# Queries and keys of retention's first head as a fifth group of the seven-product stage, by way of DRAM, and that head's retention unit in a queue of its own

## The chip, the cores and the metric

The kernel runs on one core of one Trainium2 chip. The metric is the time on the device in microseconds, the median of the runs. The kernel before: 2191.88 us, median of 3 runs (2191.68 to 2192.81). A smaller number is better.

## The reference

One transformer block on 512 tokens of width 2048, in float32. A normalized input is projected by `w_in`; the columns are the queries of eight attention heads, keys and values of three kinds, gates, and for four retention heads of width 256 queries, keys, values and gates. Sparse attention (compressed, selected and windowed keys) and retention give a mixture, which `w_out` projects; an MLP follows.

```python
h = rms_norm(x, norm_mix_pre[l])
proj = h @ w_in[l]
q_a, kv_a, gate_a, q_r, k_r, v_r, g_r = jnp.split(proj, IN_OFFSETS, axis=-1)
...
k_cmp = compress_kv(kv6[:, :, 0], cmp_pe_k[l], cmp_w1_k[l], cmp_b1_k[l], cmp_w2_k[l])
v_cmp = compress_kv(kv6[:, :, 1], cmp_pe_v[l], cmp_w1_v[l], cmp_b1_v[l], cmp_w2_v[l])
...
q_r = rope(q_r.reshape(B, S, RET_HEADS, RET_DK), pos)
k_r = rope(k_r.reshape(B, S, RET_HEADS, RET_DK), pos)
o_r = retention(q_r, k_r, v_r.reshape(B, S, RET_HEADS, RET_DV), log_gamma)
o_r = (jax.nn.silu(g_r.astype(jnp.float32)) * o_r.reshape(B, S, RET_WIDTH)).astype(x.dtype)
mix = jnp.concatenate([o_a.astype(x.dtype), o_r], axis=-1) @ w_out[l]
```

The retention heads are independent of each other: each needs the scores of its rotated queries and keys, times a decay table, then the product with its values, a normalization over its 256 outputs, and its gate.

## The kernel before, in words

Every product with a weight matrix is made of three matmuls. `split` makes of a float32 operand a rounded part (a copy on ScalarE, line 143) and a rest (a subtraction on VectorE, line 144); `mm3` (lines 155 to 157) multiplies high by high, high by low and low by high into one PSUM bank.

A projection by `w_in` is done in one of two ways.

*Direct blocks.* A block has 512 columns of `w_in`, in eight slabs (`Slab`) of 256 rows. A slab is loaded on SyncE's queue and split; `Driver.run` keeps two slabs split ahead. A step multiplies one slab into four PSUM banks, so a block is 32 pieces of six matmuls of 512 columns. After each piece the driver calls `pump`, which puts a little other work behind it; on its engine every instruction then runs in the order in which it was written. `feat_major` gives features by tokens (queries and keys, which `qk_done` copies into the tile QK), `tok_major` gives tokens by features (values and gates, `vg_done`).

*The seven-product stage.* A group is two column ranges of 256, split in two by rows and by tokens, and is computed with seven products instead of eight (Strassen's scheme in Winograd's form). `Feed` loads the quarters of the weights, sums them on VectorE (line 357) or in an accumulating DMA on GpSimd's queue (line 323), and splits them (lines 362 and 339). `groups` (line 709) runs seven products of 48 matmuls of 256 columns for a group; `in_done` puts the results together on VectorE and stores them as two halves in DRAM, `pd[n, 0]` and `pd[n, 1]`, by ScalarE's queue (line 677). The table `INC` lists the groups: one of keys and values for the compressor, one of other keys, two of attention queries.

After that stage come the direct blocks of the retention heads, queries and keys, then values and gates, for head 0 to 3 (blocks are counted from the one of values ahead of the stage, so that the first of these is block 2). Beside them, in the pumps, run the units of the object `side`: two calls of `compress` (keys, then values), loads, eight attention units (`nsa_unit`) for each of two key groups, and four retention units (`ret_unit`). A unit has two generators: the first computes scores, the second mixes. `Side.step` moves the second generator of an earlier unit and the first of a later one by one step each per piece; a first may be at most one unit ahead. A unit can be held back until the driver has reached a block (`after(n)`). `drain` runs units to their ends with no pieces between.

What a retention unit does: its first generator rotates QK on VectorE (lines 1013 to 1020, twelve operations of 128x512 in six steps), loads its decay table `dec` by GpSimd's queue (line 1023), and makes four score products into the PSUM bank `S` (line 1030), each multiplied by `dec` into the tile AT on VectorE (line 1032). Its second generator does, four times, a gate (`sg`, lines 1040 to 1043: an exponential on ScalarE, three operations on VectorE), output matmuls into the bank `oT` (line 1065), a normalization on VectorE with a power on GpSimd (lines 1069 to 1073, 161 and 162), and two transposes of the result (line 1048).

An attention unit writes each of its scores into the same single bank `S` (line 906), from where VectorE reads it (line 907, and line 897 for the compressed scores, `Pc`); then come maxima (924, 925, 931), exponentials, the scaling of the probabilities (939 to 945), transposes (970, 974) and products. `compress` transposes its position table, does 32 matmuls with the weights `w1s` (line 813) in four pieces, transposes the result (825), and makes a GELU from it on VectorE and ScalarE (the tile z, lines 826 to 838). The two halves of `w1s` have one buffer each: the value weights are loaded, by GpSimd's queue (line 799), when the matmuls with the key weights are done with a half.

GpSimd's queue starts its DMAs in the order written; each waits for its own conditions, and those behind it wait with it. The attention stage ends with the line that sets how far the driver and the units run:

```python
for blocks, units, firsts, pump in ((2, 0, 0, every), (3, 0, 0, every), (4, 7, 8, every), (5, 8, 0, every),
                                    (6, 12, 13, every), (7, 13, 0, every), (8, 22, 22, every)):
    drv.run(blocks * B - 1, pump=pump)
    side.drain(units, firsts)
    drv.run(blocks * B, pump=pump)
```

Of the kernel before, what the change touches and what calls it, by code (L numbers as in the profile page):

```python
# [10 lines left out]
F32 = mybir.dt.float32  # L11
# [5 lines left out]
P = 128  # L17
S = 512
# [5 lines left out]
HR, DR = 4, 256  # L24
# [8 lines left out]
OFF_KV = HA * DK  # L33
# [79 lines left out]
def block_kernel(ctx: ExitStack, tc: tile.TileContext, x, norm_mix_pre, w_in, cmp_pe_k, cmp_w1_k, cmp_b1_k,  # L113
# [488 lines left out]
    more = [ip.tile([P, SL], F32, name=f"half{i}") for i in range(5)]  # L602
    INC = [(OFF_KV, OFF_KV + 256), (OFF_KV + 512, OFF_KV + 1024), (0, 256), (512, 768)]
    G_KV, G_K, G_Q0, G_Q1 = range(4)
    pd = dram.tile([len(INC), 2, P, SL], F32, name="pd")

# [144 lines left out]
    drv.run()  # L751
    next_up = slabs_of(w_in, [(OFF_QR, DR), (OFF_KR, DR)], pool_a)
    for n, _ in enumerate(groups()):
# [250 lines left out]
    AT0 = [0, 512, 896, 1152]  # L1004

    def ret_unit(h):
        def scores():
            QK = RT["qk", h]
            for f in (0, 2):
                x1, x2 = QK[:, f, :], QK[:, f + 1, :]  # L1010
                t1 = rp.tile([P, S], F32, name="rt", bufs=2)
                t2 = rp.tile([P, S], F32, name="rt", bufs=2)
                nc.vector.tensor_mul(t1, x1, rot[:, 1, :])
                nc.vector.tensor_mul(t2, x2, rot[:, 1, :])
                yield
                nc.vector.tensor_mul(x1, x1, rot[:, 0, :])
                nc.vector.tensor_mul(x2, x2, rot[:, 0, :])
                yield
                nc.vector.tensor_sub(x1, x1, t2)
                nc.vector.tensor_add(x2, x2, t1)  # L1020
                yield
# [65 lines left out]
    def proj(cols, done, tok=False):  # L1087
        sl = next_up if cols[0][0] == OFF_QR else slabs_of(w_in, cols, pool_a)
        n = sum(c for _, c in cols)
        drv.steps += tok_major(sl, n, done) if tok else feat_major(sl, n // P, done)  # L1090

    for h in range(HR):
        proj([(OFF_QR + h * DR, DR), (OFF_KR + h * DR, DR)], qk_done(h))
        proj([(OFF_VR + h * DR, DR), (OFF_GR + h * DR, DR)], vg_done(h), tok=True)
    B = NSLAB
    two = lambda c: side.step() if c % 2 else None
    three = lambda c: side.step() if c else None
    every = lambda c: side.step()
    after = lambda n: (lambda: drv.at > n * B)
# [11 lines left out]
    for u in range(8):  # L1111
        if u == 4:
            side.add(*ret_unit(0), after(2), after(3))
        side.add(*nsa_unit(0, u // 2, u % 2))
    side.add(*ret_unit(1), after(4), after(5))
    for u in range(8):
        if u == 6:
            side.add(*ret_unit(2), after(6), after(7))
        side.add(*nsa_unit(1, u // 2, u % 2))
    side.add(*ret_unit(3), after(8))  # L1120
    kv_load()
    compress_load(0)
    for blocks, units, firsts, pump in ((2, 0, 0, every), (3, 0, 0, every), (4, 7, 8, every), (5, 8, 0, every),
                                        (6, 12, 13, every), (7, 13, 0, every), (8, 22, 22, every)):
        drv.run(blocks * B - 1, pump=pump)
        side.drain(units, firsts)
        drv.run(blocks * B, pump=pump)
    actx.close()
# [32 lines left out]
    for s in range(NSLAB):  # L1161
        drv.run(8 * B + s + 1, pump=lambda c: side.first() if c % 2 else None)
        if s:
# [5 lines left out]

    drv.run(10 * B - 1, pump=lambda c: side.second() if c % 2 else None)  # L1170
    side.drain()
    drv.run(12 * B)
    rctx.close()
# [8 lines left out]
    for s in range(NSLAB):  # L1182
        wend[s].load()
        drv.run(12 * B + s + 1)
    wctx.close()
# [574 lines left out]
```

## Time and profile before

| what | us |
|---|---|
| median of 3 runs | 2191.88 |
| span of the profiled execution | 2191.4 |
| TensorE busy in it | 2142.3 |
| VectorE busy | 1632.9 |
| ScalarE busy | 1018.5 |
| seven-product stage, four groups (75.0 to 231.0) | 156.0 |
| first direct block after it, queries and keys of head 0 (231.0 to 293.6) | 62.6 |
| second, values and gates of head 0 (293.6 to 355.2) | 61.6 |
| third (355.2 to 429.2) | 74.0 |
| fourth (429.2 to 496.5) | 67.3 |

The profile gives for each engine its busy time and, for each instruction, its start, its length, and what ended the idle time before it. In the rows that follow, PE is TensorE's matmul, PEld its weight load, DVE VectorE, ACT ScalarE, POOL GpSimd, SP SyncE; ACTq and POOLq are their DMA queues. A name such as `S<-QK` is output from input, and L with a number is a line of the kernel. Matmuls are pipelined, so that the listed length of one is more than its distance from the next; the rate is read from the count in a stretch of time. A direct block takes longer than its own matmuls because the units' matmuls stand between them.

### The profile page before, as it was taken

To read this page: it belongs to the slowest core of one execution; us is meant where nothing else is said; L and a number is where in the kernel's file an instruction comes from. 1 tells how busy PE (TensorE), PEld (TensorE's weight loads), DVE (VectorE), ACT (ScalarE), POOL (GpSimd) and SP (SyncE) were. 2 spreads that over 40 slices of the span, in tenths; PEclk is the share of its full clock that TensorE was granted. 3 is DMA by queue.
4 is the path that set the end of the run, shared out by engine and by line. 5 is a ranking of instruction groups with operands and counts; after the bars stand their busy time and mean duration, and the time that the engine had idled before them with its cause. 6 is when DMAs were issued, how large, how long until landed. Compare 5 with 4: busy or idle time off the path is not lost.

```text
span 2191.4 us, 33442 instructions
## 1 busy us (share of the span) xinstructions
PE 2142.3 (98%) x13363; PEld 1921.7 (88%) x13363; DVE 1632.9 (75%) x1925; ACT 1018.5 (46%) x1469; POOL 153.2 (7%) x175
## 2 busy tenths in 40 slices
PE   8999999999999999999999999999999999999996
PEld 7999887778778899999999999999888888888875
DVE  6987346656665543588888877777878999999997
ACT  5544233333433323475554555555664454445453
POOL 1000210010000000000000000000000000000011
PEclk9999999999999999999999999999999999999998
DMA  6876842243223334577877757676785657567575
GB/s 193 214 199 167 278 126 64 75 106 97 60 78 115 107 102 134 175 237 202 231 220 204 210 163 205 167 206 185 226 240 161 209 154 219 161 187 207 167 232 110
DMA packets 275310, 372.15 MB, mean 170 GB/s; under 512 B 16683, under 2 KB 190811, under 8 KB 274001
## 3 DMA queue, kind: packets, MB, share of 16 engines
q1 hardware_dynamic: 209040, 265.00, 38.6%
q0 software_dynamic: 38736, 59.91, 14.8%
q10 hardware_dynamic: 27378, 45.11, 5.6%
q8 instruction: 105, 1.72, 0.3%
q14 instruction: 51, 0.42, 0.1%
HBM read 321.92 MB, written 48.04 MB: 169 GB/s over the span
## 4 chain that ended last, share of the span: by engine, by line
PE 86%; DVE 7%; DMA 3%; ACT 2%; issue 2%; POOL 0%; SPq 0%; DVEq 0%; ACTq 0%; POOLq 0%
PE prod L156 17%; PE prod L157 17%; PE prod L155 17%; PE mm L155 10%; PE mm L157 10%; PE mm L156 10%; DVE wlo L339 2%; PE S L906 2%; DMA raw<-in_w_in 1%; PE S L1030 1%; PE PT L970 1%; PE oT L1065 1%; PE oT L813 1%; PE oT L155 1%; DMA xh<-ud 1%
## 5 line engine op out<-in xcount | busy, mean ns | idle before, releaser
L362 ACT CAST whi<-Y 128x1024 fp32r<-128x1024 f32 x227 | 238.2, 1050 | 282.1 <-PE prod L157 118.4
L156 PE MATMUL prod<-wlo,Hh 128*128 128x512 f32 x896 | 350.3, 391 | 4.4 <-DVE wlo L339 4.3
L155 PE MATMUL prod<-whi,Hh 128*128 128x512 f32 x896 | 349.4, 390 | 1.4 <-ACT whi L362 1.4
L362 ACT CAST whi<-low 128x1024 fp32r<-128x1024 f32 x215 | 226.3, 1054 | 267.1 <-PE prod L157 135.7
L157 PE MATMUL prod<-whi,Hl 128*128 128x512 f32 x896 | 349.3, 390 | 0.0
L339 DVE TENSOR_TENSOR wlo<-Y,whi 128x1024 fp32r<-128x1024 f32 x227 | 276.7, 1220 | 52.3 <-ACT whi L362 51.4
L339 DVE TENSOR_TENSOR wlo<-low,whi 128x1024 fp32r<-128x1024 f32 x215 | 262.0, 1220 | 56.0 <-ACT whi L362 55.3
L157 PE MATMUL prod<-Hh,wlo 128*128 128x256 f32 x1024 | 284.6, 278 | 4.9 <-DVE wlo L339 4.9
L155 PE MATMUL prod<-Hh,whi 128*128 128x256 f32 x1024 | 285.0, 278 | 0.3 <-ACT Hh L143 0.3
L156 PE MATMUL prod<-Hl,whi 128*128 128x256 f32 x1024 | 284.2, 278 | 0.9 <-DVE Hl L144 0.9
L155 PE MATMUL mm<-whi,Hh 128*128 128x416 f32 (+4 forms) x704 | 264.2, 375 | 0.7 <-ACT Hh L143 0.7
L157 PE MATMUL mm<-whi,Hl 128*128 128x416 f32 (+4 forms) x704 | 248.5, 353 | 0.7 <-DVE Hl L144 0.7
L156 PE MATMUL mm<-wlo,Hh 128*128 128x416 f32 (+4 forms) x704 | 247.7, 352 | 0.0
L144 DVE TENSOR_TENSOR wlo<-raw,whi 128x1024 fp32r<-128x1024 f32 (+4 forms) x120 | 129.3, 1083 | 157.2 <-ACT whi L143 156.5
L155 PE MATMUL prod<-sx,whi 128*128 128x256 f32 x768 | 212.2, 276 | 0.0
L157 PE MATMUL prod<-sx,wlo 128*128 128x256 f32 x768 | 212.2, 276 | 0.0
L156 PE MATMUL prod<-sx,whi 128*128 128x256 f32 x768 | 212.2, 276 | 0.0
L143 ACT CAST whi<-raw 128x1024 fp32r<-128x1024 f32 (+4 forms) x120 | 111.9, 936 | 205.3 <-PE mm L157 104.9
L156 PEld LDWEIGHTS prod<-wlo,Hh 128*128 128x128 f32 x896 | 168.6, 188 | 42.5 <-DVE wlo L339 7.6
L155 PEld LDWEIGHTS prod<-whi,Hh 128*128 128x128 f32 x896 | 168.5, 188 | 37.1 <-ACT whi L362 1.9
L157 PEld LDWEIGHTS prod<-whi,Hl 128*128 128x128 f32 x896 | 168.6, 188 | 34.7
L157 PEld LDWEIGHTS prod<-Hh,wlo 128*128 128x128 f32 x1024 | 193.0, 188 | 5.6 <-DVE wlo L339 5.5
(321 smaller groups left out, 4420.9 us busy)
## 6 DMA issues: line engine op xcount, KB each, us to landing
low<-in_w_up SPq DMA_DIRECT2D x76, 512.0 KB, 4.8
raw<-in_w_in SPq DMA_DIRECT2D x144, 256.0 KB, 3.1
Y<-in_w_up SPq DMA_DIRECT2D x64, 512.0 KB, 4.8
low<-in_w_down SPq DMA_DIRECT2D x64, 512.0 KB, 4.9
Y<-in_w_down SPq DMA_DIRECT2D x64, 512.0 KB, 4.7
Y<-ud SPq DMA_DIRECT2D x49, 512.0 KB, 8.1
ud<-Y ACTq DMA_DIRECT2D x77, 256.0 KB, 5.2
half<-in_w_in SPq DMA_DIRECT2D x27, 512.0 KB, 4.8
```

The costliest lines, as they stand in the source:

```text
L143: nc.scalar.copy(hi, src)
L144: nc.vector.tensor_sub(lo, src, hi.bitcast(F32))
L155: nc.tensor.matmul(ps, ah, bh, start=first, stop=False, skip_group_check=more)
L156: nc.tensor.matmul(ps, ah, bl, start=False, stop=False, skip_group_check=more)
L157: nc.tensor.matmul(ps, al, bh, start=False, stop=last, skip_group_check=more)
L339: nc.vector.tensor_sub(lo, src, hi.bitcast(F32))
L362: nc.scalar.copy(hi, src)
L813: nc.tensor.matmul(hid[:65, :DK], kv[:, l:l + STRIDE * 64 + 1:STRIDE], w1s[l // 16][:, l % 16, :], start=l == 0, stop=l == CBLK - 1)
L906: nc.tensor.matmul(sps[:, :c + L], QT[g][:, h, qs], k, start=True, stop=True)
L970: nc.tensor.transpose(pt[:, e * P:(e + 1) * P], Pt[:, e, rows_of(j)], ident)
L1030: nc.tensor.matmul(sps[:, :n], QK[:, 2 + d, rows_of(j)], QK[:, d, j * P:], start=d == 0, stop=d == 1)
L1065: nc.tensor.matmul(o[:, :DR], AT[:, a0:a0 + P], vr[:, j, :], start=j == 0, stop=j == i)
```

## The change

Queries and keys of head 0 become the fifth entry of `INC` and go through the seven-product stage; the direct block for them goes, and every later block has a number less by one. The result comes back from DRAM by two loads on GpSimd's queue (`qk_load`), called ahead of the first block, behind the loads of the compressor's key weights. The retention unit of head 0 leaves `side` and is the only unit of a second queue, `front`, which is moved by one step after each piece too, from the first piece on; its first eight steps do nothing. Its outputs may begin when the block of its values is done, as before. The table of the last loop is written anew for the lower block numbers, with a pair for `front.drain`.

```diff
-    INC = [(OFF_KV, OFF_KV + 256), (OFF_KV + 512, OFF_KV + 1024), (0, 256), (512, 768)]
-    G_KV, G_K, G_Q0, G_Q1 = range(4)
+    INC = [(OFF_KV, OFF_KV + 256), (OFF_KV + 512, OFF_KV + 1024), (0, 256), (512, 768), (OFF_QR, OFF_KR)]
+    G_KV, G_K, G_Q0, G_Q1, G_R0 = range(5)
...
-    next_up = slabs_of(w_in, [(OFF_QR, DR), (OFF_KR, DR)], pool_a)
+    next_up = slabs_of(w_in, [(OFF_VR, DR), (OFF_GR, DR)], pool_a)
...
+    def qk_load():
+        QK = RT["qk", 0] = rp.tile([P, 4, S], F32, name="QK")
+        for j in range(2):
+            nc.gpsimd.dma_start(QK[:, 2 * j:2 * j + 2, :].rearrange("p f n -> p (f n)"), pd[G_R0, j])
+
     def ret_unit(h):
         def scores():
             QK = RT["qk", h]
+            if not h:
+                for _ in range(8):
+                    yield
...
     for h in range(HR):
-        proj([(OFF_QR + h * DR, DR), (OFF_KR + h * DR, DR)], qk_done(h))
+        if h:
+            proj([(OFF_QR + h * DR, DR), (OFF_KR + h * DR, DR)], qk_done(h))
         proj([(OFF_VR + h * DR, DR), (OFF_GR + h * DR, DR)], vg_done(h), tok=True)
...
-    every = lambda c: side.step()
+    front = Side()
+
+    def every(c):
+        side.step()
+        front.step()
+
...
     for u in range(8):
-        if u == 4:
-            side.add(*ret_unit(0), after(2), after(3))
         side.add(*nsa_unit(0, u // 2, u % 2))
-    side.add(*ret_unit(1), after(4), after(5))
+    side.add(*ret_unit(1), after(3), after(4))
...
+    front.add(*ret_unit(0), lambda: True, after(2))
     kv_load()
     compress_load(0)
...
+    qk_load()
+    for blocks, units, firsts, early in ((2, 0, 0, (0, 0)), (3, 0, 0, (0, 1)), (4, 0, 0, (1, 0)), (5, 11, 12, (1, 0)),
+                                         (6, 12, 0, (1, 0)), (7, 21, 21, (1, 0))):
+        drv.run(blocks * B - 1, pump=every)
+        front.drain(*early)
         side.drain(units, firsts)
-        drv.run(blocks * B, pump=pump)
+        drv.run(blocks * B, pump=every)
```

The rest of the diff lowers block numbers in the same way.

The change moves instructions on several engines. First GpSimd, from the loads of the compressor's key weights (`w1s` from `in_cmp_w_k`) or just behind them to the first attention unit's loads; `dec` is head 0's decay table. Before:

```order
L799 DMA w1s<-in_cmp_w_k 128x16x128 x2
L792 DMA pes<-in_cmp_pe_v 32x128
L794 DMA b1s<-in_cmp_b_v 128x1
L796 DMA w2s<-in_cmp_w_v 128x128
L799 DMA w1s<-in_cmp_w_v 128x16x128 x2
L863 DMA Vh<-vd 128x2048
L863 DMA Vl<-vd 128x2048
L858 DMA kT<-pd 128x2x512
L859 DMA kT<-pd 128x1024
L875 DMA BT<-rd 16x4x512 x8
L868 DMA qT<-pd 128x1024 x2
L1023 DMA dec<-in_c_dec 128x512
```

And in the changed kernel:

```order
L1009 DMA QK<-pd 128x1024 x2
L792 DMA pes<-in_cmp_pe_v 32x128
L794 DMA b1s<-in_cmp_b_v 128x1
L796 DMA w2s<-in_cmp_w_v 128x128
L799 DMA w1s<-in_cmp_w_v 128x16x128 x2
L1031 DMA dec<-in_c_dec 128x512
L863 DMA Vh<-vd 128x2048
L863 DMA Vl<-vd 128x2048
L858 DMA kT<-pd 128x2x512
L859 DMA kT<-pd 128x1024
L875 DMA BT<-rd 16x4x512 x8
L868 DMA qT<-pd 128x1024 x2
```

The load of QK stands ahead of the value side of the compressor, and `dec` has moved from behind the first attention loads to the place right behind the value weights.

Second VectorE, in the first block after the stage, where the compressor's key side ends (`b1s` and `z`), in the changed kernel, from the last operation of the rotation on:

```order
L1028 TENSOR_TENSOR QK<-QK,rt 128x512
L826 TENSOR_TENSOR b1s<-b1s,PT 128x1
L828 TENSOR_SCALAR z<-PT,b1s 128x63
L830 TENSOR_TENSOR z<-z 128x63
L1040 TENSOR_TENSOR AT<-S,dec 128x512
L832 TENSOR_SCALAR z<-z 128x63
L833 TENSOR_TENSOR z<-z 128x63
L1040 TENSOR_TENSOR AT<-S,dec 128x384
L144 TENSOR_TENSOR wlo<-raw,whi 128x1024
```

Before, the operations on `z` stood here with the weight split alone. The two rows that write AT come from a place 50 pieces later, and so do the score products on TensorE that they read: the first stands 15 pieces into the block, with one piece between it and the second.

Third VectorE, at the scores of the first attention unit (lines 907 and 897). Before:

```order
L144 TENSOR_TENSOR wlo<-raw,whi 128x1024
L907 SCALAR_TENSOR_TENSOR Pt<-S,BT 128x128
L897 SCALAR_TENSOR_TENSOR Pc<-S,BT 128x7
L144 TENSOR_TENSOR wlo<-raw,whi 128x1024
L907 SCALAR_TENSOR_TENSOR Pt<-S,BT 128x128
L897 SCALAR_TENSOR_TENSOR Pc<-S,BT 128x7
L907 SCALAR_TENSOR_TENSOR Pt<-S,BT 128x128
```

And in the changed kernel, from the end of the second gate (`sg`) on:

```order
L1050 RECIPROCAL sg<-sg 128x256
L1051 TENSOR_TENSOR gr<-gr,sg 128x256
L907 SCALAR_TENSOR_TENSOR Pt<-S,BT 128x128
L897 SCALAR_TENSOR_TENSOR Pc<-S,BT 128x7
L144 TENSOR_TENSOR wlo<-raw,whi 128x1024
L907 SCALAR_TENSOR_TENSOR Pt<-S,BT 128x128
L897 SCALAR_TENSOR_TENSOR Pc<-S,BT 128x7
L1077 BN_STATS rst<-rn 128x6
L1078 BN_AGGR rst<-rst 128x2
```

Head 0's gates and normalizations now stand between the weight split and the first score, and between the scores; before, they stood behind unit 3, beside the scores of unit 4.

More of the change, by code (lines that the diff above doesn't have):

```diff
@@ L1087, in proj @@
     def proj(cols, done, tok=False):
-        sl = next_up if cols[0][0] == OFF_QR else slabs_of(w_in, cols, pool_a)
+        sl = next_up if cols[0][0] == OFF_VR else slabs_of(w_in, cols, pool_a)
         n = sum(c for _, c in cols)
@@ L1111, in block_kernel @@
     for u in range(8):
-        if u == 4:
-            side.add(*ret_unit(0), after(2), after(3))
         side.add(*nsa_unit(0, u // 2, u % 2))
-    side.add(*ret_unit(1), after(4), after(5))
+    side.add(*ret_unit(1), after(3), after(4))
     for u in range(8):
         if u == 6:
-            side.add(*ret_unit(2), after(6), after(7))
+            side.add(*ret_unit(2), after(5), after(6))
         side.add(*nsa_unit(1, u // 2, u % 2))
-    side.add(*ret_unit(3), after(8))
+    side.add(*ret_unit(3), after(7))
+    front.add(*ret_unit(0), lambda: True, after(2))
     kv_load()
     compress_load(0)
-    for blocks, units, firsts, pump in ((2, 0, 0, every), (3, 0, 0, every), (4, 7, 8, every), (5, 8, 0, every),
-                                        (6, 12, 13, every), (7, 13, 0, every), (8, 22, 22, every)):
-        drv.run(blocks * B - 1, pump=pump)
+    qk_load()
[3 more added lines that the diff above has]
+        front.drain(*early)
         side.drain(units, firsts)
-        drv.run(blocks * B, pump=pump)
+        drv.run(blocks * B, pump=every)
     actx.close()
@@ L1161, in block_kernel @@
     for s in range(NSLAB):
-        drv.run(8 * B + s + 1, pump=lambda c: side.first() if c % 2 else None)
+        drv.run(7 * B + s + 1, pump=lambda c: side.first() if c % 2 else None)
         if s:
@@ L1167, in block_kernel @@
     mx.close()
-    drv.run(10 * B - 1, pump=lambda c: side.second() if c % 2 else None)
+    drv.run(9 * B - 1, pump=lambda c: side.second() if c % 2 else None)
     side.drain()
-    drv.run(12 * B)
+    drv.run(11 * B)
     rctx.close()
@@ L1183, in block_kernel @@
         wend[s].load()
-        drv.run(12 * B + s + 1)
+        drv.run(11 * B + s + 1)
     wctx.close()
```

## The prediction

> **What bounds the kernel now.** I read the page first, then the busy times by stretches, then the order of events on TensorE, VectorE and GpSimd around the places that the change touches.
>
> ```profile
> span 2191.4 us, 33442 instructions
> PE 2142.3 (98%) x13363; PEld 1921.7 (88%) x13363; DVE 1632.9 (75%) x1925; ACT 1018.5 (46%) x1469; POOL 153.2 (7%) x175
> ...
> PE 86%; DVE 7%; DMA 3%; ACT 2%; issue 2%; POOL 0%; SPq 0%; DVEq 0%; ACTq 0%; POOLq 0%
> ```
>
> TensorE is busy for 98% of the span, and the chain that ended last runs through it for 86%. So a matmul that goes is worth its full time, and a wait that comes in front of one costs its full time. The profiled span, 2191.4 us, is 0.5 below the median of the runs, 2191.9; my sum is a difference on the span, and I add it to the median.
>
> ```profile
> 192.90:231.06 38.16, 38.16 (x339) 38.16 (x337) 24.79 (x23) 15.12 (x16) 6.85 (x9) 1.00 0.53 141
> 697.57:713.89 16.32, 16.32 (x74) 13.52 (x72) 13.00 (x17) 5.06 (x5) 0.00 (x0) 1.00 0.70 225
> ```
>
> Two stretches (length, then busy us and count of PE, PEld, DVE, ACT, POOL; granted clock; DMA share; GB/s). The first is the last group of the seven-product stage: 336 matmuls of 256 columns begin in it (the view also counts three that cross its edges), in 38.16 us, with TensorE never idle and VectorE at 65%. The second is a piece of a direct block with nothing between: 72 matmuls of 512 columns in 16.32 us. I call six of these a **piece** (one weight slab into one of four result tiles): 16.32/12 = 1.36 us. A block is 32 pieces, 43.5 us.
>
> **The change, term by term.** *Matmuls.* One direct block (192 matmuls, 43.5 us) goes, one group (336, 38.16 us) comes: **-5.4 us**. The group's sums, splits and loads lie under it as they do in the stretch shown, where neither VectorE nor DMA (0.53) was full.
>
> *Round trip through DRAM.* The two halves of QK are stored, loaded, and rotated on VectorE while TensorE does the first 15 pieces of the next block (I keep the clock of before, where that block begins at 231.1).
>
> ```profile
> pd<-da ACTq DMA_DIRECT2D x4, 512.0 KB, 6.1
> KV<-pd POOLq DMA_DIRECT2D x2, 512.0 KB, 6.6
> kT<-pd POOLq DMA_DIRECT2D x2, 512.0 KB, 13.3
> 231.98 0.33 ACTq L677 DMA_DIRECT2D pd<-da  x1
> 260.40 0.47 PE L155 MATMUL mm<-Hh,whi 128*128 128x512 f32 x1
> L1013 DVE TENSOR_TENSOR rt<-QK,rot 128x512 f32<-128x512 f32 x8 | 5.4, 680 | 0.0
> ```
>
> The last store goes out at 232.0 and takes about 6.1, the load 6.6 to 13.3: QK is there between 245 and 252. Rotating is 12 operations of 0.68, with one weight split of 1.2 among them, 9.4 us, so it ends between 254 and 262. TensorE comes to the first score of the retention head (line 1038 after) at 260.4. The split among them is needed only five pieces later still. I cost this at **0**: the wait of the next term, at the same place, covers some 5 us of lateness, and what exceeds that would be paid in full.
>
> *The decay table behind the compressor's weights.* This is the step I trust least to be free. The order of GpSimd puts the load of dec (c_dec) behind the second load of the compressor's value weights, which waits until TensorE has used the key weights.
>
> ```profile
> 259.43 1.16 POOL L799 DMA_DIRECT2D w1s<-in_cmp_w_v  x1 [4.88 <-PE oT L813]
> 260.57 0.57 POOL L863 DMA_DIRECT2D Vh<-vd  x1
> w1s<-in_cmp_w_v POOLq DMA_DIRECT2D x2, 1024.0 KB, 7.5
> Vh<-vd POOLq DMA_DIRECT2D x1, 1024.0 KB, 8.7
> raw<-in_w_in SPq DMA_DIRECT2D x144, 256.0 KB, 3.1
> 356.73 1.88 PE L1030 MATMUL S<-QK 128*128 128x512 f32 x4
> 358.05 0.80 PE L155 MATMUL mm<-Hh,whi 128*128 128x512 f32 x1
> 265.52 0.43 PE L842 MATMUL PT<-z,w2s 128*128 128x63 f32 x2 [0.79 <-DVE z L838]
> ```
>
> So dec takes the place that Vh has now, 260.6. The weights land at 259.4 + 7.5 = 266.9; Vh, a megabyte issued right behind, lands at 260.6 + 8.7 = 269.3, 2.4 later. A quarter of a megabyte in that place lands near 267.5, and the product with dec (0.7, as a rotation step) ends at 268.2. The first score takes TensorE from 260.4 to 261.7 (358.05 - 356.73 = 1.32), the next piece to 263.1, and the second score needs the one bank S, free only after that product: a wait of 5.1. A wait of 0.79 that stands there now (the compressor's z) falls into it: **+4.3 us**. Ends: with a load that is not held up (raw, also 256 KB, 3.1) 0.5; with the slowest load shown (kT, 13.3) 10.7. I take 4.3, since Vh is the nearest row.
>
> The Trainium skill speaks against this wait: DMA: Bandwidth & Descriptors, section Anatomy of one DMA, fits one transfer from GpSimd's queue at 2.0 us plus bytes/436e3, by which dec would land 2.6 us after its issue (an estimate from that page), this term would be near 0.3 and the sum 4 lower. The trace does not agree for transfers queued behind others: by the same fit a megabyte takes 4.4 us, and the rows above have 7.5 and 8.7.
>
> *Two users of VectorE at once.* Retention's outputs of head 0 now run in the same pieces as the first two attention units. Head 1 before shows the retention part alone, at the end of its block, where it also will stand:
>
> ```profile
> 501.89 0.42 DVE L1069 BATCH_NORM_STATS2 rst<-rn 128x6 f32<-128x256 f32 x1
> ...
> 504.26 0.29 DVE L1041 TENSOR_SCALAR sg<-sg 128x256 f32<-128x256 f32 x1
> ...
> 506.71 1.22 DVE L144 TENSOR_TENSOR wlo<-raw,whi 128x1024 fp32r<-128x1024 f32 x1
> 499.20 0.60 PE L1065 MATMUL oT<-vr,AT 128*128 128x256 f32 x2
> 503.75 1.03 PE L1065 MATMUL oT<-vr,AT 128*128 128x256 f32 x4
> 508.97 1.46 PE L1065 MATMUL oT<-vr,AT 128*128 128x256 f32 x6
> 299.10 0.43 PE L906 MATMUL S<-kT,qT 128*128 128x160 f32 x2
> 300.75 0.43 PE L906 MATMUL S<-kT,qT 128*128 128x160 f32 x2
> 299.56 0.29 DVE L907 SCALAR_TENSOR_TENSOR Pt<-S,BT 128x128 f32<-128x128 f32 x1 [2.92 <-PE S L906]
> 303.11 0.41 DVE L925 TENSOR_REDUCE nst<-Pt 128x2 f32<-128x256 f32 x1
> 309.06 0.88 DVE L945 TENSOR_SCALAR Pt<-Pt,nst 128x128 f32<-128x128 f32 x4
> 308.88 0.51 PE L906 MATMUL S<-kT,qT 128*128 128x160 f32 x2
> 310.61 0.60 PE L970 MATMUL PT<-misc,Pt 128*128 128x128 f32 x4
> ```
>
> A gate is 2.45 us (504.26 to 506.71), a normalization 2.4 (501.89 to 504.26). After the first output matmul (499.20) VectorE has 7.5 us of this queued: normalization and second gate end at 506.71. In the changed order that matmul stands two pieces ahead of unit 0's first score, at 299.10 - 2.72 = 296.4, so VectorE is free at 303.9. The score is read by 304.3 (0.29, and about half of that for its compressed part), and only then may the second score use bank S; it would be due at 300.75 + 0.25 (the output matmul) = 301.0. **Wait 3.3.** Carrying VectorE's order on from 304.3: split 1.22, score 0.44, normalization 2.4, score and maxima 0.9 (0.29, 0.41 and a smaller one), gate 2.45, score and maximum 0.7, normalization 2.4, split 1.22, score 0.44: 316.4, where unit 1's second score may go. TensorE would come at 304.3 + 8.13 (300.75 to 308.88) + 2.5 for two outputs (1.03 and 1.46) = 314.9: **wait 1.5.** Then a gate and the scaling of unit 0's probabilities, 2.45 + 1.2 (0.88 and two small ones), to 320.0, while the transposes are due at 316.4 + 1.7 = 318.1: **wait 1.9.** Together **+6.7 us**.
>
> *Relief at the old place, and the heir to it.*
>
> ```profile
> 374.69 0.91 PE L906 MATMUL S<-kT,qT 128*128 128x384 f32 x2 [1.12 <-DVE Pt L907]
> 401.00 1.23 PE L970 MATMUL PT<-misc,Pt 128*128 128x128 f32 x4 [0.63 <-DVE Pt L945]
> 402.83 0.94 PE L906 MATMUL S<-kT,qT 128*128 128x416 f32 x2 [0.60 <-DVE Pc L897]
> 404.99 0.60 PE L970 MATMUL PT<-misc,Pt 128*128 128x128 f32 x4
> ```
>
> Where head 0 stands now, TensorE waits 1.12 + 0.63 + 0.60, and four transposes take 1.23 instead of 0.60: 3.0 in all, which go: **-3.0** (ends -1.2, the two shorter ones alone, and -3.6, double the 0.63). The 1.12 is also the low end of the term before, as the wait of this kind that the kernel already shows; its high end is 9, one gate more. But with a block fewer, head 1 takes over the pattern, outputs among the four scores of the next unit. The same carrying on gives waits of 0.6, 1.1 and 1.2, of which the second is the 1.12 seen; I take **+2.5** (ends 1.1 and 3). The matmuls of the retention head are the same in both places; heads 2 and 3 keep their order against the pieces.
>
> Sum: -5.4 + 0 + 4.3 + 6.7 - 3.0 + 2.5 = **+5.1 us**; 2191.9 + 5.1 = **2197.0**. The waits eat the saved matmuls.
>
> **Rivals.** (a) *It is hidden anyway, and the change is faster.* The table lands early and VectorE's queue costs no more than at the old place: -5.4 + 0.5 + 1.1 - 3.0 + 1.1 = -5.7, 2186.2. For it speaks that VectorE has room on the mean (75%), against it that a queue in order blocks by what stands ahead, not by its mean. It decides at bank S: if two gates are not ahead of the first score's reader, there is no wait. (b) *The table lands early*, with VectorE as summed: 0.5 instead of 4.3, +1.3, 2193.2. (This is what the Trainium skill's fit, cited above, would give.) Against it: Vh, Vl and kT all land in order. (c) *The table is late, VectorE's queue is harmless*: -5.4 + 4.3 + 1.1 - 3.0 + 1.1 = -1.9, 2190.0. (d) *The extra megabyte delays the weight slabs.*
>
> ```profile
> 235.00:240.00 5.00, 5.00 (x24) 4.14 (x23) 0.00 (x0) 0.00 (x0) 0.00 (x0) 1.00 1.04 362
> ```
>
> The DMA engines are full there (1.04 at 362 GB/s), so QK's megabyte adds 2.9 us of transfers; if slabs wait for it, TensorE does: +8.0, 2199.9. Against it: QK can only start when its store has landed, near 238, and slabs three and four are then in flight ahead of it.
>
> **How the numbers follow.** Chances: forecast 0.55, (a) 0.13, (b) 0.13, (c) 0.10, (d) 0.09. The bound for a difference that a measurement of this kernel tells from none is 0.2%, 4.4 us: under 2187.5 faster, over 2196.3 slower. The forecast's own range, from its ends, is 2191 to 2202; of its 0.55, 0.33 lies above 2196.3, 0.21 within, 0.01 below. (b) is within but for 0.02, (c) within but for 0.02 below, (a) faster, (d) slower. So faster 0.16, within 0.40, slower 0.44. The range to hold 8 in 10: 2187 to 2202, which leaves out most of (a) and the far end of the dec term.
>
> **What would show it.** The first block right after the stage begins about 38.2 later than now, and 32 pieces fewer stand behind. GpSimd's row for dec follows the second w1s of the values; on TensorE the second row of S<-QK has a wait on DVE AT of 4 to 5 us. On VectorE a gate and a normalization stand ahead of unit 0's first score, and TensorE's S rows there wait for DVE Pt, 3.3 and 1.5 us, the transposes for Pt 1.9. The rows at 374.69 and 401.00 lose their waits. The forecast is wrong if dec lands within 3 us of issue, if the S rows of unit 0 show no wait, or if the rotation ends after dec.

## The result, and the profile after

| kernel | median, us | lowest to highest | runs |
|---|---|---|---|
| before | 2192.35 | 2191.68 to 2194.16 | 4 |
| changed | 2207.95 | 2207.78 to 2208.87 | 4 |

The ratio is 1.0069, with a 95% interval from 1.0057 to 1.0082: the change makes the kernel slower by 15.6 us. The prediction had slower as the likeliest, but by 5.1 us, and its range ended at 2202. (Its base, 2191.88, is the median of the first three runs of the kernel before.)

The page of the changed kernel (span; busy time and share of each engine; the chain that ended last by engine):

```profile
span 2206.1 us, 33752 instructions
PE 2139.5 (97%) x13507; PEld 1925.6 (87%) x13507; DVE 1650.3 (75%) x1942; ACT 1024.5 (46%) x1474; POOL 157.0 (7%) x179
...
PE 83%; DVE 8%; issue 3%; DMA 2%; ACT 2%; POOL 1%; SPq 0%; DVEq 0%; ACTq 0%; POOLq 0%
```

TensorE is busy for 2.8 us less, and still the span is 14.7 longer, so it stands for 17.5 us more. In the chain TensorE's share is 83% where it was 86%; VectorE, GpSimd and issue have one point more each.

The order of events in the changed kernel at the places that the prediction named (start, length, engine and line, operation, shape, and in brackets the idle time before it and what ended that):

```profile
286.28 0.69 DVE L1021 TENSOR_TENSOR rt<-QK,rot 128x512 f32<-128x512 f32 x1 [0.34 <-DMA QK<-pd]
...
294.55 0.68 DVE L1028 TENSOR_TENSOR QK<-QK,rt 128x512 f32<-128x512 f32 x1
...
299.41 1.17 POOL L799 DMA_DIRECT2D w1s<-in_cmp_w_v  x1 [5.63 <-PE oT L813]
300.57 0.56 POOL L1031 DMA_DIRECT2D dec<-in_c_dec  x1
310.37 0.69 DVE L1040 TENSOR_TENSOR AT<-S,dec 128x512 f32<-128x512 f32 x1 [9.36 <-DMA dec<-in_c_dec]
311.12 2.93 PE L1038 MATMUL S<-QK 128*128 128x384 f32 x4 [7.80 <-DVE AT L1040]
...
353.52 0.41 DVE L1080 TENSOR_SCALAR rn<-rn,rst 128x256 f32<-128x256 f32 x1 [0.68 <-POOL rst L162]
354.63 1.75 DVE L1050 RECIPROCAL sg<-sg 128x256 f32<-128x256 f32 x1
356.82 0.29 DVE L907 SCALAR_TENSOR_TENSOR Pt<-S,BT 128x128 f32<-128x128 f32 x1
357.33 0.51 PE L906 MATMUL S<-kT,qT 128*128 128x160 f32 x2 [3.01 <-DVE Pc L897]
370.42 0.51 PE L906 MATMUL S<-kT,qT 128*128 128x160 f32 x2 [2.20 <-DVE Pc L897]
373.48 0.82 PE L970 MATMUL PT<-misc,Pt 128*128 128x128 f32 x4 [1.16 <-DVE Pt L945]
...
428.12 1.22 PE L970 MATMUL PT<-misc,Pt 128*128 128x128 f32 x4 [0.89 <-DVE Pt L945]
429.95 0.94 PE L906 MATMUL S<-kT,qT 128*128 128x416 f32 x2 [0.61 <-DVE Pc L897]
...
514.65 0.49 PE L906 MATMUL S<-kT,qT 128*128 128x128 f32 x2 [0.91 <-DVE Pt L907]
540.37 0.82 PE L970 MATMUL PT<-misc,Pt 128*128 128x128 f32 x4 [0.92 <-DVE Pt L945]
653.65 0.44 PE L1056 MATMUL PT<-misc,rn 128*128 128x128 f32 x2 [1.38 <-DVE rn L1081]
```

The mechanisms are those of the prediction: QK is back at 286.3, and its rotation ends at 295.2, 4.8 us before the first score reads it (300.0); the table is what VectorE waits for, and TensorE behind it; beside units 0 and 1 the score's reader (356.82) stands behind a normalization and a gate. Three things differ. The dec wait is 7.80, not 5.1. The rows that were to lose their waits (401.00 and 402.83 before) have them still, at 428.12 and 429.95. And head 2 has a wait of its own at 653.65.

Stretches of the changed kernel (length; busy us and count of PE, PEld, DVE, ACT, POOL; granted clock; DMA share; GB/s):

```profile
76.00:80.00 4.00, 4.00 (x24) 4.00 (x23) 3.50 (x3) 2.07 (x3) 2.01 (x3) 0.57 1.26 336
303.30:311.10 7.80, 0.01 (x1) 0.00 (x0) 0.73 (x2) 0.00 (x0) 0.15 (x1) 0.83 1.05 353
311.10:315.00 3.90, 3.88 (x7) 2.48 (x8) 1.21 (x4) 1.19 (x2) 0.00 (x0) 0.50 0.72 284
357.30:361.00 3.70, 3.67 (x19) 3.20 (x20) 2.40 (x7) 1.07 (x3) 0.55 (x1) 1.00 0.41 91
```

After the wait of 7.8 TensorE works at half its clock for 3.9 us; after the wait of 3.0 at 357 it does not in this profile. So the price of the dec wait is more than its length.

The wait of 3.0 is not safe from it either. A second profile of the same kernel (e8 below) has the same wait, and half clock behind it; so has that of e1:

```profile
354.24 0.87 PE L906 MATMUL S<-kT,qT 128*128 128x160 f32 x2 [3.01 <-DVE Pc L897]
```

```profile
353.90:357.25 3.35, 3.01 (x9) 2.57 (x10) 1.61 (x5) 0.37 (x1) 0.00 (x0) 0.50 0.25 58
357.30:361.00 3.70, 3.70 (x19) 3.10 (x19) 2.89 (x10) 1.83 (x9) 0.55 (x1) 1.00 0.40 127
```

```profile
348.40:351.75 3.35, 3.35 (x12) 2.77 (x10) 1.61 (x6) 1.16 (x3) 0.55 (x1) 0.50 0.69 197
```

(The first row and the two stretches below it are from e8, the last stretch from e1.) Of the six profiles with this wait, five have the half clock behind it (e1, e7, e8, e12, x1); the one of the result has not.

**Where the 14.7 us are.** TensorE's pieces have the same order in both kernels, so the starts of equal pieces can be subtracted. A block is 32 pieces, 43.5 us; head 0's scores (3.4 us of TensorE) and outputs (5.0) lie in other pieces than before and are taken out. Where the old place of head 0 falls away, the work beside the pieces moves forward by 20 pieces, and by 12 more at head 1; from there on pieces are compared that have the same work beside them, and a piece that is missing counts 1.36.

| stretch | predicted | measured in the first profile |
|---|---|---|
| a group for a block | -5.4 | -2.8 |
| round trip of QK | 0 | 0 |
| first block after the stage: the table | +4.3 | +8.9 |
| next 14 pieces: outputs beside units 0 and 1 | +6.7 | +8.0 |
| relief at the old place | -3.0 | -3.4 |
| behind it, up to head 1 | 0 | +0.3 |
| head 1, the heir | +2.5 | +3.0 |
| head 2 | 0 | +0.8 |
| sum | +5.1 | +14.8 (the span: +14.7) |

The 2.6 that the first row misses are no part of the change, but for some 0.4. The stage with five groups ended between 37.4 and 40.7 later than in the profile of before in fifteen profiles of the changed kernel and its variants (mean 39.0), and in four profiles with four groups it varied from 230.7 to 232.4 (mean 231.5): the group costs 38.5 on the mean, where 38.16 was predicted. One source of the spread is the first row of stretches above, a stretch of half clock behind a 1.9 us gap at 73; it appears in some profiles of either order (here in that of y2, a kernel with the order of before, again at 76):

```profile
76.00:80.00 4.00, 4.00 (x24) 4.00 (x23) 3.48 (x4) 1.84 (x2) 1.67 (x3) 0.59 1.28 327
```

The 8.0 beside units 0 and 1 is the low end of what other profiles show. In e1, e7, e8, e12 and x1, where the order there is the same, these 14 pieces cost 9.2 to 11.6. The waits in them are no longer (5.5 to 6.2 together, 6.4 in the first profile); what is added is 3.4 to 10.2 us of half clock.

### The profile page after: what moved, and what is told of

The parts are those of the page before. It is cut to its first block, busy times and chain, and to the rows that moved or that the text cites. A ratio compares the mean times of both kernels' runs of the same rounds, so it can differ in the third digit from the quotient of the medians.

```text
span 2206.1 us, 33752 instructions
## 1 busy us (share of the span) xinstructions
PE 2139.5 (97%) x13507; PEld 1925.6 (87%) x13507; DVE 1650.3 (75%) x1942; ACT 1024.5 (46%) x1474; POOL 157.0 (7%) x179
## 4 chain that ended last, share of the span: by engine, by line
PE 83%; DVE 8%; issue 3%; DMA 2%; ACT 2%; POOL 1%; SPq 0%; DVEq 0%; ACTq 0%; POOLq 0%
PE prod L157 16%; PE prod L156 16%; PE prod L155 16%; PE mm L155 10%; PE mm L157 9%; PE mm L156 9%; DVE wlo L339 2%; PE S L906 1%; PE S L1038 1%; DMA out<-Y 1%; PE PT L970 1%; PE oT L1073 1%; DVE wlo L144 1%; DMA xh<-ud 1%; PE oT L155 1%
## 5 line engine op out<-in xcount | busy, mean ns | idle before, releaser
L144 DVE TENSOR_TENSOR wlo<-raw,whi 128x1024 fp32r<-128x1024 f32 (+4 forms) x112 | 119.4, 1072 | 140.7 <-ACT whi L143 140.4
L156 PEld LDWEIGHTS prod<-Hl,whi 128*128 128x128 f32 x1024 | 193.0, 189 | 1.1 <-DVE Hl L144 1.1
```

The costliest lines, as they stand in the source:

```text
L144: nc.vector.tensor_sub(lo, src, hi.bitcast(F32))
L156: nc.tensor.matmul(ps, ah, bl, start=False, stop=False, skip_group_check=more)
```

## The experiments

The runs below come from six chips; the kernel before was run on each, with medians of 2193.2 to 2194.5 us, and the ratios are to it on the same chip. A ratio's interval is some 2 us wide to each side, so a difference of 1 or 2 us between two runs is not clear of the noise. The first part of a run's name (e1, x1, y1) stands for it below, and "on e1" means with the edit of e1.

### The changed kernel again

> The changed kernel as it is, for a value on the same chip as the others and for another profile of the seven-product stage, which took 40.6 more than before in two profiles and 38.6 in three, where 38.2 was expected. If the 2 us belong to single executions (a stretch of lower granted clock near 76 us), this profile may show either, and the time is 2207 to 2210.

Measured: 2209.45, ratio 1.0070 (1.0056 to 1.0083). Its stage ended 37.4 after before's, 3.3 earlier than in the first profile, and its waits are nearly the same (7.28 for 7.80 at the table, 3.01, 2.05 and 1.17 beside units 0 and 1). The 3.3 come back behind the stage, mostly as two stretches of half clock, at 354 and at 429, that the first profile does not have.

### The table: earlier, on another queue, later, with nothing behind it

```diff
 def qk_load():
     ...
+    dec = RT["dec", 0] = rp.tile([P, S], F32, name="dec")     # e1
+    nc.gpsimd.dma_start(dec, c_dec[:, 0, :])
```

> Only the load of head 0's decay table is moved: it goes out right behind the two loads of QK, ahead of the compressor's value weights. Theory (the queue of GpSimd holds the table up): the wait of 7.8 us in front of the second score of head 0 goes, the small wait for the compressor's z (0.8) comes back, and the time is 2200 to 2201.5, some 7 us under the changed kernel's 2208. Rival (VectorE is what is late there, with the rotation and the compressor's z ahead of the score's reader, and the table only ends last by a little): the wait shrinks by less than 3 us, 2205 or more.

Measured: 2199.11, ratio 1.0019 (1.0010 to 1.0028): 10 us under the changed kernel, more than theory said. The second score has no wait left, and the compressor's wait of 0.8, which was expected back, stays away:

```profile
303.04 1.46 PE L1043 MATMUL S<-QK 128*128 128x384 f32 x4
```

Over the first block the gain is 10.1: the wait of 7.8, and the half clock behind it, under which this same score took 2.93 instead of 1.46.

```diff
-            nc.gpsimd.dma_start(dec, c_dec[:, h, :])
+            (nc.gpsimd if h else nc.scalar).dma_start(dec, c_dec[:, h, :])     # e7
```

> Only the load of head 0's decay table is moved to ScalarE's queue, at the same place of the program. Theory (it is late because GpSimd's queue issues and lands in order, behind the compressor's weights): it lands some 3 to 4 us after its issue, the wait of 7.8 us goes down to 1 or less, and the time is 2199 to 2201.5, as with the table loaded first. Rival (the DMA engines are full with the weights' small packets, whatever the queue): it lands 7 us or more after its issue, and the time is 2206 or more.

Measured: 2199.96, ratio 1.0023 (1.0014 to 1.0033). Issue on ScalarE's queue and use on VectorE:

```profile
298.00 0.35 ACTq L1031 DMA_DIRECT2D dec<-in_c_dec  x1
301.22 0.69 DVE L1040 TENSOR_TENSOR AT<-S,dec 128x512 f32<-128x512 f32 x1 [0.97 <-PE S L1038]
```

VectorE waited for the score, not for the table, which was there within 3.2 us, from the same memory and beside the same weights. On this queue it also went out earlier, 0.65 us ahead of the second half of the weights instead of 1.16 behind it:

```profile
298.65 1.17 POOL L799 DMA_DIRECT2D w1s<-in_cmp_w_v  x1 [5.63 <-PE oT L813]
```

So the run shows what the queue and the earlier issue are worth together; it does not separate them. The Trainium skill (DMA: Bandwidth & Descriptors, section Issuing engines are not separate DMA queues) says that starting DMAs from several engines saves only the time of issuing, since all run on the same 16 DMA engines. Here it saved 9.5 us of run time (2209.45 to 2199.96, on one chip), for a small load that otherwise stood in a queue among megabytes.

What in the queue holds it up? First the keys, 1 MB, were put ahead of the table:

```diff
+            if not h:
+                k_load()                                    # e12; loads() leaves it out
             dec = rp.tile([P, S], F32, name="dec")
```

> The changed kernel, with the two loads of the attention keys (512 KB each) moved ahead of the load of head 0's table on GpSimd's queue. Theory (what stands ahead in the queue lands first, and then the table): it lands 2.5 us later (two times the 1.25 between the keys' landings in the changed kernel), the wait goes from 7.8 to 10.3, the stretch of half clock behind it stays as long, and the time is 2.5 us over the changed kernel's 2209.5 on this chip: 2211 to 2213. Rival (the table takes its 9 us because the engines are full, whatever is ahead of it in the queue): no change, 2208.5 to 2210.

Measured: 2208.95, ratio 1.0068 (1.0055 to 1.0082): no change. The rival held, and my picture of the queue, first what stands ahead and then the table, fell. The edit takes the megabyte from behind the table as well as putting it ahead, so it shows that a megabyte weighs the same on either side, not that one ahead weighs nothing. Then the 3 MB behind the table were taken away:

```diff
 def loads():
-    k_load()
     load_bias(0)
     q_load(0)
+    k_load()
+    v_load()                                                # x1; compress(1) leaves it out
```

> The changed kernel, with the loads of values and keys (4 loads, 3 MB) moved from right behind head 0's table to behind the first bias and query loads, which wait until the compressor's value weights have been used. Theory (loads that stand behind in the queue share the engines with those ahead, 2.6 MB were moved in the 10 us in which 1 MB landed): the weights' half lands 5 to 6 us after its issue instead of 9.7, the table 1 us later, the wait falls from 7.8 to 3 or 4 us, and the time is 4 us or more under 2209: 2203 to 2205.5. Rival (the weights' half takes its time by itself): the wait stays at 7 or more and the time at 2207 to 2210.

Measured: 2205.92, ratio 1.0048 (1.0036 to 1.0061), by the ratios some 4.5 us under the changed kernel. The wait is 4.45, a little over what was expected. Landing times (issues of DMA: size, us from issue to landing) in the changed kernel, then in x1 with VectorE's and TensorE's rows, then the same half of the weights in the kernel before:

```profile
w1s<-in_cmp_w_v POOLq DMA_DIRECT2D x1, 1024.0 KB, 9.7
dec<-in_c_dec POOLq DMA_DIRECT2D x1, 256.0 KB, 9.7
```

```profile
w1s<-in_cmp_w_v POOLq DMA_DIRECT2D x1, 1024.0 KB, 6.9
dec<-in_c_dec POOLq DMA_DIRECT2D x1, 256.0 KB, 6.4
...
304.15 0.69 DVE L1038 TENSOR_TENSOR AT<-S,dec 128x512 f32<-128x512 f32 x1 [6.01 <-DMA dec<-in_c_dec]
304.90 2.93 PE L1036 MATMUL S<-QK 128*128 128x384 f32 x4 [4.45 <-DVE AT L1038]
```

```profile
w1s<-in_cmp_w_v POOLq DMA_DIRECT2D x1, 1024.0 KB, 7.3
```

So the 3 MB behind the table on its queue delay it by 3 us. With e12 this fits transfers of the queue that are under way together and share full DMA engines (share 1.05 at 353 GB/s in the stretch of the wait, in which 2.75 MB moved, while of this queue's loads only the weights' half and the table, 1.25 MB, had landed at its end). One thing stays open: the weights' half lands after 9.5 to 9.7 only where the table and then the values follow it (both profiles of the changed kernel, e2, e4), and after 6.7 to 7.4 in e1, e7, e12 and before, where a larger load follows directly. The runs do not say why. The half clock followed the wait of 4.45 too: the score in x1's last row takes 2.93 again.

### Head 0's outputs: where, how fast, without gates

```diff
+    head0 = ret_unit(0)
     for u in range(8):
+        if u == 4:
+            side.add(nothing, head0[1], lambda: True, after(2))     # e2; the drain table counts one unit more
         side.add(*nsa_unit(0, u // 2, u % 2))
...
-    front.add(*ret_unit(0), lambda: True, after(2))
+    front.add(head0[0], nothing)
```

> Head 0's scores stay in the queue beside the compressor; its outputs go back to the place behind the fourth attention unit. Theory (outputs and the first two attention units share VectorE, about 8 us): these go, the waits at the old place (3.0) come back, and head 1 has its old pattern (1.7 less): 2208 - 8.3 + 3.0 - 1.7 = 2201, the dec wait unchanged at 7 to 8. Rival (the old place costs as much as the new one, since a retention unit beside attention units is dear wherever it stands): 2206 to 2209.

Measured: 2207.27, ratio 1.0056 (1.0043 to 1.0068): 2 us, where 7 were expected; it lies in the rival's range. The 8.0 beside units 0 and 1 went, but nearly all came back later. As I read the order, which no run tests by itself, the outputs push every later unit behind when they stand in the row of the units, and a block of pieces to stand behind is missing at the end. New waits appear, the last at 690 us, with half clock behind it:

```profile
411.04 0.94 PE L906 MATMUL S<-kT,qT 128*128 128x416 f32 x2 [1.32 <-DVE Pc L897]
692.69 0.78 PE L970 MATMUL PT<-misc,Pt 128*128 128x128 f32 x2 [2.65 <-DVE Pt L945]
```

> Both edits together. Theory (the two costs lie at different places and add): 2208 - 7 - 7 = 2194, with 1.5 either way; so equal to the kernel before within what can be measured, and still not the 5.4 below it that the matmuls are worth. Rival (with the table early the outputs or the compressor become what is late): 2198 or more.

Measured: 2196.84, ratio 1.0010 (1.0001 to 1.0019). The two edits add, but as 10 and 2 instead of 7 and 7, so the time lies above the 2192.5 to 2195.5 expected.

```diff
             def gate(i):
+                if not h:
+                    return                                  # e4
```

> The changed kernel with the gates of head 0 left out (their exponentials and the three operations on VectorE, four times 2.45 us; the outputs of that head are multiplied by the raw gate values). Theory (VectorE's queue in order sets the waits of the first two attention units): the waits of 3.0, 2.2 and 1.2 us go down to 1 us in all and the time falls by 5 to 7 us, to 2201 to 2203. Rival (the waits come from TensorE's own order and the banks, or from ScalarE's copies, not from VectorE's work): less than 2 us, 2206 or more.

Measured: 2203.10, ratio 1.0036 (1.0023 to 1.0048), 6.4 under the changed kernel, and the same 6.4 in the 14 pieces of units 0 and 1, where 1.6 is left (its profile and the changed kernel's first one both have the full clock there). The 9.8 us of VectorE that were left out were not on TensorE's path by themselves; they were in front of the score's reader.

```diff
     def every(c):
         side.step()
-        front.step()
+        if not front.a or c % 2:                            # e6, on e1: outputs at half rate
+            front.step()
```

> The table first, and head 0's outputs stepped after every second piece instead of every one, so that they lie beside units 0 to 3. Theory (VectorE's work per piece sets the waits): of 8 us some 4 stay, 2194 to 2196.5. Rival (each output costs its 2 us wherever it stands): 2198 to 2200.

Measured: 2193.05, ratio 0.9992 (0.9983 to 1.0000): 6 us under e1, better than expected, and equal to the kernel before within what can be told. Not all of it is waits: over the 32 pieces of units 0 to 3 e6's profile is 6.7 us shorter than e1's, but 4.2 shorter than the changed kernel's first one, which has the full clock there as e6's has; the rest is half clock in e1's profile. Only two waits over 1 us are left beside units 0 to 3:

```profile
346.12 0.46 PE L906 MATMUL S<-kT,qT 128*128 128x128 f32 x2 [1.29 <-issue]
353.94 0.51 PE L906 MATMUL S<-kT,qT 128*128 128x160 f32 x2 [1.32 <-DVE nst L939]
```

In e5, also on e1, the outputs wait 20 steps more, and for the bank `oT` to be free of a unit. They were meant for units 2 to 6; in the profile the four stand beside the scores of units 4 to 7 (388.8, 406.0, 425.5 and 446.1 us).

> The table first, and head 0's outputs 20 steps later, one to each of the attention units 2 to 6 instead of all four beside units 0 and 1. Theory (VectorE's queue is too full beside the first units, where a piece has little other TensorE work in it): the 8 us of waits there go and at most 2 come back at the new places, so 5 to 7 us under the 2199 of the table alone: 2192 to 2194. Rival (each output costs its 2 us beside any unit): 2197 to 2199.

Measured: 2195.01, ratio 1.0002 (0.9993 to 1.0011): 4 us under e1, a little less than expected. Both say that the same work costs less where it is spread over more pieces.

### What is left: VectorE's gates?

Two replacements of the reciprocal, both on e6, and a control:

```diff
-                nc.vector.tensor_scalar_add(e, e, 1.0)      # e9, and e11 on the kernel before
-                nc.vector.reciprocal(e, e)
+                nc.scalar.activation(e, e, AF.Ln, bias=1.0)
+                nc.scalar.activation(e, e, AF.Exp, scale=-1.0)
...
-                nc.vector.reciprocal(e, e)                  # e13
+                nc.gpsimd.tensor_tensor(e, e, mhalf[:, 0:1].to_broadcast([P, DR]), op=ALU.pow)
+                nc.scalar.activation(e, e, AF.Square)
```

> Table first, outputs of head 0 at half rate, and in the gates of all four heads the addition and the reciprocal on VectorE (0.28 and 1.75 us, sixteen times) replaced by a logarithm and an exponential on ScalarE. Theory (what is still lost lies in VectorE's queue beside the retention outputs, of head 0 and of head 1 that follows it): each gate is 2.0 us shorter for VectorE, the 3.6 us left beside units 0 to 3 and the 3.0 of head 1 shrink to half or less, and the time is 2188.5 to 2190.5, under the kernel before by 0.2 to 0.3%. Rival (ScalarE, which now has three functions in turn in each gate, delays the splits' copies, or pays for changing functions): 2193 or more.

> A control: the kernel before with the same shorter gates. Theory: it has less to win, the 1.1, 0.6 and 0.6 us of waits beside head 0's outputs and what head 1 to 3 lose to the gates: 1 to 3 us, 2191.5 to 2193.5 on this chip, so that the changed order with the table first and half rate is then ahead by 2 to 3 us. Rival (the gates cost the kernel before as much): 2189 or less, or, with ScalarE's functions changing, over 2195.

> Table first, outputs of head 0 at half rate, and in the gates of all heads the reciprocal (1.75 us on VectorE, sixteen times) replaced by a power of minus one half on GpSimd and a square on ScalarE. Theory (what is left beside the outputs is VectorE's queue): 2 to 4 us less than with half rate alone (2193), so 2189 to 2191. Rival (GpSimd takes so long for 256 columns of powers, 0.55 us for one column now, that gates come late to the outputs, and the power of the normalization waits behind them): 2195 or more.

Measured: e9 2194.15, ratio 1.0001 (0.9993 to 1.0010); e11 2196.61, 1.0013 (1.0004 to 1.0021); e13 2833.03. The rivals held: ScalarE changes its functions twice for each gate, and GpSimd needs 41 us for 256 columns of powers (min/median/max ns in the second row).

```profile
L1054 ACT ACT_TABLE_LOAD x15 | 19.2, 1283 | 0.3
L1055 ACT ACT_TABLE_LOAD x15 | 19.2, 1283 | 0.3
```

```profile
L1055 POOL TENSOR_TENSOR sg<-sg,misc x16: 41138/41140/41163, 336.7 to 1374.3; 128x256 f32<-128x256 f32 x16
```

So neither could test the theory. Leaving all gates out does:

> Table first, head 0's outputs at half rate, and no gates in any head (the outputs are multiplied by the raw gate values; 16 exponentials and 48 operations on VectorE, 39 us of it, are left out). Theory (what is still lost is VectorE's queue): the waits beside units 0 to 3 and head 1's outputs go to 1 us in all, 5 to 7 us under the 2193 with gates: 2186 to 2188. Rival (what is left is in the pieces, the banks or TensorE's order): 2191 or more.

> The kernel before without gates in any head, the control of the run above. Theory: its waits beside head 0's outputs (1.1 and 0.6, twice) and some slower pieces go, 2 to 4 us under 2194: 2190 to 2192. Then the changed order, with its two costs taken away, is ahead by about the 5.4 us of its matmuls.

Measured: x2 (on e6) 2189.26, ratio 0.9978 (0.9968 to 0.9988); x3 2193.44, 0.9994 (0.9985 to 1.0003). The theory was half right: 3 of the 5 to 7 us went. The control gained some 1 us, with no change within its interval, where 2 to 4 were expected; so without gates the changed order is ahead by 3.5 to 4 us, not by the 5.4 of its matmuls. Head 1's heir stayed. VectorE there, in x2:

```profile
497.30 0.43 DVE L1083 BATCH_NORM_STATS2 rst<-rn 128x6 f32<-128x256 f32 x1 [1.86 <-ACT rn L1081]
498.87 0.41 DVE L1086 TENSOR_SCALAR rn<-rn,rst 128x256 f32<-128x256 f32 x1 [0.74 <-POOL rst L162]
499.67 0.28 DVE L907 SCALAR_TENSOR_TENSOR Pt<-S,BT 128x128 f32<-128x128 f32 x1
500.00 0.49 PE L906 MATMUL S<-kT,qT 128*128 128x128 f32 x2 [1.53 <-DVE Pt L907]
```

VectorE is not full: it stands, 1.86 for ScalarE's copy of the outputs and 0.74 for GpSimd's power, and the score's reader stands behind it. That is the blocking of a queue in order, without a gate in it, shown at this one place. The last edit keeps all work and cuts it over the three steps of an output: statistics and power, then the two products and half a gate, then the other half.

```diff
                 inv_root(st[:, 9:10], st[:, 7:8], st[:, 8:9], 1, 1.0)
-                nc.vector.tensor_scalar(n, n, ...)
-                nc.vector.tensor_mul(n, n, gr[:, i, :])
                 if held is not None:
                     place(*held)
                 yield
+                nc.vector.tensor_scalar(n, n, ...)
+                nc.vector.tensor_mul(n, n, gr[:, i, :])
                 if i + 1 < NT:
-                    gate(i + 1)
+                    gate(i + 1, 0)
                 held = (i, n)
                 yield
+                if i + 1 < NT:
+                    gate(i + 1, 1)
                 yield
```

> Table first, half rate, and in every head the same VectorE work of an output cut over its three steps: statistics and power in the first, the normalization's two products and half a gate in the second, the other half in the third (at most 2 us of VectorE in a step instead of 2.45, and no waiting for GpSimd's power ahead of a score's reader). Theory (the length of what stands in VectorE's queue ahead of the score's reader sets the waits): 2 to 4 us under half rate alone (2193): 2189 to 2191, faster than the kernel before by 0.15 to 0.25%. Rival (the amount of work counts, not how it is cut): 2192 to 2194.

> The kernel before with the same finer steps, as control. Theory: it loses less to these waits, so it gains 1 to 2 us: 2192 to 2193.5 on this chip.

> Table first, finer steps, head 0's outputs after every piece as in the changed kernel. Theory: of the 8 us beside units 0 and 1, 3 to 5 go: 2194 to 2196 where the table alone gave 2199. Rival: 2198 to 2200.

Measured: y1 (on e6) 2192.25, ratio 0.9994 (0.9985 to 1.0003), no gain over e6; y2 2196.49, 1.0007 (0.9998 to 1.0015), no gain; y3 (on e1) 2195.70, 1.0006 (0.9997 to 1.0015), 3 us under e1. For y1 and y2 the theory missed; y1 lies in the rival's range. Where the queue is crowded, cutting helps: the 14 pieces of units 0 and 1 take 2.0 us less in y3 than in the changed kernel's first profile, at the full clock in both (4.4 less than in e1's, which has two stretches of half clock there). Where the work is spread already, it does not show in the time: at head 1 it saves 0.7 us, and at head 2 it costs 1.1.

Of the versions that compute the reference, e6 and y1 have the lowest times; their intervals hold no change or come within 0.01% of it, and none beats the kernel before by 0.2%.

## Why the prediction was wrong, point by point

*Matmuls, -5.4: right but for 0.4.* A group costs 38.5 on the mean of the profiles and a block 43.5. What single executions add in the stage, up to 2.5, varies in the kernel before too (by 1.8 in four profiles).

*Round trip, 0: right.* QK's rotation ended at 295.2 and the first score needed it at 300.0.

*The table, +4.3: the mechanism right, the size half.* This is the step that failed. It put the table in the place of Vh, landing 0.6 us after a weights' half that lands 7.5 after its issue. The half landed after 9.7 and the table another 1.2 later, so the wait was 7.8 instead of 5.1. x1 shows 3 us of that lateness as the price of the 3 MB that follow; but in the kernel before the same megabytes follow the half, and it took 7.3, so why it is slower with the table between them stays open. Then came the half clock, which the prediction did not have at all: with it the 7.8 became the 10.1 that e1 won back. Against this, 1.2 came back in the same block, where the compressor's wait of 0.79 and one of 0.53 for a weight split (at 243.40 before) are gone. Net 8.9. The term's own upper end, 10.7, would have held it; but with it the sum is 2203.4, and with the upper ends of all terms 2208.0, and the range stopped at 2202.

The Trainium skill (TensorE: Matmul & The Clock Gate, section Part 1: The HAM clock gate) says that the clock is halved after an idle window of about 3.4 us and that the windows run free. The rows agree in part. The stretches of half clock behind these waits are 3.4 us long, or two or three times that, and the same wait has one behind it in some executions and not in others, as the 3.01 has and the gap of 1.9 at 73. But a wait need not be as long as a window: 3.01 is shorter than 3.4, and so is the 2.65 of e2 and e3, which had one too. Here the measurement decides. Behind all six waits of 4.45 or more at the table the clock was 0.50.

*VectorE's queue, +6.7: right in the waits.* Waits of 3.3, 1.5 and 1.9 were expected, 3.01, 2.20 and 1.16 came. They cost 8.0 in the first profile and up to 11.6 in others, where the half clock follows them; that the prediction did not have here either. e4 confirms the gates and e6 the pace as the cause of the waits.

*Relief, -3.0: right by number, not by reason.* 3.4 went from the pieces ahead of 398 us, among them the wait of 1.12; what the rest was, the rows do not show. The other two waits named, 0.63 and 0.60, are still there in the new profile (0.89 and 0.61), and so are the 1.23 of the four transposes (1.22): they belong to the attention units, not to the retention head beside them.

*Heir, +2.5: right,* 3.0. *"Heads 2 and 3 keep their order": not quite.* Head 2's outputs come a piece earlier behind its scores, which costs 0.8.

*The rivals.* (a) to (c) needed a table or a queue that costs little; e1, e4 and e6 show what each is worth when it is taken away. (d), QK's megabyte delaying slabs, did not happen: with the table first, the first block is 1.2 shorter than before, once the scores are taken out.

## What to carry to other kernels

Before moving a small load into a queue with large ones, ask what stands behind it as well as ahead, and whether another engine's queue is free: here that one word was worth 9.5 us. A wait of TensorE of some 3 us should be priced with the slow stretch that may stand behind it, and one profile of it is not enough: the same wait had one in five profiles of six. Work that an engine in order does beside a chain with a single buffer (here the bank of the scores) costs by what stands in front of the chain's reader, its own waits included, not by its mean share: 8 us or more at full rate, under 4 spread over twice as many pieces.

## What the runs showed of the hardware that was not expected

- All six waits of 4.45 to 7.80 us at the table had TensorE's granted clock at 0.50 behind them. A wait of 3.01 had it in five profiles of six, one of 2.65 in both profiles with it (e2, e3), one of 2.59 not (y3). These stretches of half clock lasted 3.4 us, or two or three times that.
- 256 KB on GpSimd's queue, behind a megabyte of weights, took 6.4 to 9.7 us to land, with the order of the landings kept; on ScalarE's queue, issued 0.65 us ahead of the same weights, at most 3.2.
- A reciprocal of 128x256 on VectorE takes 1.75 us, an addition of the same shape 0.28; a power of 128x256 on GpSimd takes 41.1 us, while one column takes 0.55.
- A logarithm between exponentials on ScalarE cost two loads of function tables of 1.28 us in each gate.
